# A product-key expert layer on one core: gate tiles stored and read in pieces, read a group ahead, and four early activation tiles kept for the end of the gates

## The chip, the cores and the metric

The kernel runs on one core of a Trainium2 chip. The metric is the device time of one execution in microseconds (us). A core has a matrix engine (PE), a vector engine (DVE), a scalar engine (ACT), a general engine (POOL) and a queue engine (SP) that issues most DMAs. All engines take their instructions in order and wait on semaphores. PE writes to PSUM; everything else here lives in SBUF or, as scratch, in HBM.

## The reference

One decoder layer over 512 tokens of width 1024: a gated token mixer, then an expert network with 16,384 experts, then a last norm. The change touches only the expert network. For each token and each of 8 heads, two small key searches give 16 expert indices and 16 softmax weights.

```python
idx = jnp.take_along_axis(cand_i, pos, axis=-1)
g = jax.nn.softmax(top_s, axis=-1)
u_sel = jnp.take(expert_u, idx, axis=0)
act = jax.nn.gelu(jnp.einsum('thkd,td->thk', u_sel, xc).astype(jnp.float32))
v_sel = jnp.take(expert_v, idx, axis=0)
return jnp.einsum('thk,thkd->td', (g * act).astype(xc.dtype), v_sel)
```

## The kernel before

The first 500 us are the mixer, which the change leaves alone. Of the 512 tokens, 384 (three blocks of 128) go through a dense form of the expert network and 128 through row gathers.

**Dense form.** The experts are cut into 128 tiles of 128. `act_tile(j)` multiplies tile j of `ut` (expert_u transposed, 512 KB) with the normed tokens: 24 matmuls of 384 columns, then a gelu on ACT. `out_tile(j)` takes these activations, multiplies them on DVE with the gates of the tile (`L638`), splits the product into a high and a low part (`w_hi` on ACT, `w_lo` on DVE), loads the expert_v part of `uv` (512 KB) and adds 18 matmuls of 512 columns to the six accumulators that stand in PSUM through all 128 tiles. Every weight passes `weights()`: a load into one of four `raw` buffers, `whi` on ACT (`L74`), `wlo` on DVE or POOL (`L75`), each with three buffers.

**Gates.** The softmax weights are turned into a dense matrix tokens x 16,384 in 48 blocks of 8 tokens: one-hot matrices on DVE (`rows_of`, `L564` and `L566`), 16 matmuls on PE, an eviction on ACT into `stg` (`L585`). After each 4 blocks, 32 tokens, the whole `stg` of 2 MB goes to HBM (`gscr`, `L592`). The second stage reads the gates back by expert tile: `gt` holds all 384 tokens for `JG` = 4 tiles, 768 KB, in runs of 4 x 32 tokens x 4 bytes = 512 bytes (`L634`). Two `gt` buffers stand in turn, and the read stands in the code at the first tile that needs it.

**Tiles ahead of the gates.** `NL` = 74 of the activation tiles (the list `LAG`) don't need the gates and are made earlier, so that PE has work while DVE searches and builds one-hots: `AR` = 20 in the key search, `AD` = 4 after the decode of each of three token blocks, and the other 42 spread over the 48 gate blocks. The first 12 stay in SBUF (`keep`), the other 62 are written to HBM (`ascr`) and read back (`back`, `L661`) `PRE` = 2 tiles ahead into `PRE` + 2 buffers of 192 KB. `wlo` of the first 20 is made on POOL, of the others on DVE.

**Gathers.** For the last 128 tokens, `gathered(i)` reads 128 rows of 8 KB (1 MB) by an indirect DMA of POOL (`L402`), and DVE makes a dot product and a weighted sum. 24 of the 128 steps are spread over the gate blocks, the rest over the second stage.

**Order.** The program is written tile by tile, but a scheduler sets the order on each engine by its own estimates; DMAs of SP go out in that order, one queue, each waiting for its buffer and for the DMA eight places before it, whose semaphore it uses again. The second stage is the loop over j in 0 to 128: `read_back`, `act_tile` where it wasn't made before, `out_tile` of the tile before, and a share of the gathers. At its end `finish` norms the three token blocks.

Of the kernel before, what the change touches and what calls it, by code (L numbers as in the profile page):

```python
# [11 lines left out]
F32 = mybir.dt.float32  # L12
F32R = mybir.dt.float32r
F16 = mybir.dt.float16
BF16 = mybir.dt.bfloat16
I32 = mybir.dt.int32
U32 = mybir.dt.uint32
AF = mybir.ActivationFunctionType
# [3 lines left out]
P = 128  # L22
D = 1024
S = 512
KD = D // P
# [7 lines left out]
NT = ND // P  # L33
EPS = 1e-6
TE = 8
TG = 32
NG = ND // TG
JG = 4
NL = 74
LAG = [j for j in range(P) if j * NL // P != (j - 1) * NL // P]  # L40
JK = 12
GSC = 32768.0
# [3 lines left out]
NS = 2  # L46
AR = 20
AD = 4
UP = 24
PRE = 2  # L50
C_VEC = dict(nm=0, nf=8, ca=16, rw=40, rb=80, brg=90, big=100, lam=110)
NVEC = 120

# [2 lines left out]
def layer(ctx: ExitStack, tc: tile.TileContext, a):  # L56
# [21 lines left out]
    def weights(src, k, eng=None):  # L78
        raw = ring.tile([P, k * P], F32, tag="raw", name="raw", bufs=4)
        SP.dma_start(raw, src)  # L80
        hi, lo = split(raw, [P, k * P], ("whi", "wlo"), ring, 3, eng)
        return hi.rearrange("p (k m) -> p k m", k=k), lo.rearrange("p (k m) -> p k m", k=k)
# [28 lines left out]
    gscr = dram.tile([NG, P, P, TG], F32, name="gscr")  # L111
# [255 lines left out]
    kept = {}  # L367

    def act_tile(j):
        u = weights(a["ut"][j], KD, G if j in LAG[:AR] else V)  # L370
        pa = bank("01", (P, S))
        mm3(pa[:, :ND], u, n2d)
        if j in LAG[:JK]:
            g = gp.tile([P, ND], F32, tag="keep", name="keep", bufs=JK)
        else:
            g = gp.tile([P, ND], F32, tag="gel", name="gel", bufs=3)
        A.activation(g, pa[:, :ND], AF.Gelu_apprx_tanh)
        return g
# [3 lines left out]
    def lag_tiles(n):  # L382
        for _ in range(n):
            j = next(ahead_of_gates, None)
            if j is None:
                return
            kept[j] = act_tile(j)
            if j not in LAG[:JK]:
                SP.dma_start(ascr[j], kept[j])
# [9 lines left out]
    def gathered(i, pin=False):  # L399

        r = gp.tile([P, 2 * D], F32, tag="row", name="row", bufs=4)
        ins = G.indirect_dma_start(  # L402
            out=r, out_offset=None, in_=a["uv"], in_offset=bass.IndirectOffsetOnAxis(ap=uidx[:, i : i + 1], axis=0)
        )
        if pin:
            tc.keep_in_program_order(ins)
        junk = gp.tile([P, D], BF16, tag="junk", name="junk", bufs=1)
        tc.keep_in_program_order(
            V.scalar_tensor_tensor(junk, r[:, :D], 1.0, n2tok, op0=ALU.mult, op1=ALU.mult, accum_out=dots[:, i : i + 1])  # L409
        )  # L410
        A.activation(dots[:, i : i + 1], dots[:, i : i + 1], AF.Gelu_apprx_tanh)
        A.activation(dots[:, i : i + 1], dots[:, i : i + 1], AF.Copy, scale=gk[:, i : i + 1])
        if lastrow:
            gathered_sum()
        lastrow.append((i, r))
# [135 lines left out]
    with tc.tile_pool(name="gates", bufs=1) as rp:  # L551

        ioR = rp.tile([P, P, 2], F16, name="ioR")
        G.iota(ioR, pattern=[[1, P], [0, 2]], base=0, channel_multiplier=0, allow_small_or_imprecise_dtypes=True)
        TP = TE // 2

        def rows_of(t, t0):
            def bc(x):
                return x[:, t0 : t0 + TE].rearrange("p (q t) -> p q t", t=2).unsqueeze(2).to_broadcast([P, TP, P, 2])

            e12 = rp.tile([P, 2, TP, P, 2], F16, tag="e12", name="e12", bufs=2)
            ehl = rp.tile([P, 2, TP, P, 2], F16, tag="ehl", name="ehl", bufs=2)
            for s in range(2):
                V.tensor_tensor(e12[:, s], ioR.unsqueeze(1).to_broadcast([P, TP, P, 2]), bc(iT[t][:, s]), op=ALU.is_equal)  # L564
            for s in range(2):
                V.tensor_mul(ehl[:, s], e12[:, 0], bc(gT[t][:, s]))  # L566
            return e12[:, 1], ehl[:, 0], ehl[:, 1]

        blocks = [(t, t0) for t in range(NT) for t0 in range(0, P, TE)]
        ahead = rows_of(*blocks[0])  # L570
        for n, (t, t0) in enumerate(blocks):
            e2, eh, el = ahead
            if n + 1 < len(blocks):
                ahead = rows_of(*blocks[n + 1])
            c, s0 = divmod(t0, TG)
            if s0 == 0:
                stg = rp.tile([P, P, TG], F32, tag="stg", name="stg", bufs=2)
            for q4 in range(TE // 4):
                pg = bank("4567")
                for i in range(4):  # L580
                    o = pg[:, i * P : (i + 1) * P]
                    ti = 4 * q4 + i
                    T.matmul(o, e2[:, ti // 2, :, ti % 2], eh[:, ti // 2, :, ti % 2], start=True, stop=False)  # L583
                    T.matmul(o, e2[:, ti // 2, :, ti % 2], el[:, ti // 2, :, ti % 2], start=False, stop=True)  # L584
                A.activation(  # L585
                    stg[:, :, s0 + 4 * q4 : s0 + 4 * q4 + 4],
                    pg.rearrange("p (t i) -> p i t", t=4),
                    AF.Copy,
                    scale=1.0 / GSC,
                )  # L590
            if s0 + TE == TG:
                SP.dma_start(gscr[t * (P // TG) + c], stg)  # L592
            left = NL - AR - AD * NT
            lag_tiles((n + 1) * left // len(blocks) - n * left // len(blocks))
            for i in range(n * UP // len(blocks), (n + 1) * UP // len(blocks)):
                gathered(i)


    ep = ctx.enter_context(tc.tile_pool(name="exp", bufs=1))
# [9 lines left out]
                acc[t][k // 4][:, c : c + P], hk[:, t * P : (t + 1) * P], ident, start=False, stop=False, skip_group_check=True  # L609
            )  # L610

    def finish(t, parts):
        sq = ep.tile([P, S], F32, tag="fsq", name="fsq", bufs=2)
        ss = ep.tile([P, 2], F32, tag="fss", name="fss", bufs=2)
        A.activation(sq, parts[0], AF.Square, accum_out=ss[:, 0:1])
        A.activation(sq, parts[1], AF.Square, accum_out=ss[:, 1:2])
        s1 = ep.tile([P, 1], F32, tag="fs1", name="fs1", bufs=2)
        V.tensor_add(s1, ss[:, 0:1], ss[:, 1:2])
        A.activation(s1, s1, AF.Sqrt, bias=epst, scale=1.0 / D)
        V.reciprocal(s1, s1)  # L620
        o = ep.tile([P, D], F32, tag="fo", name="fo", bufs=2)
        for f in range(2):
            fs = slice(f * S, (f + 1) * S)
            V.scalar_tensor_tensor(o[:, fs], parts[f], s1, gfin[:, fs], op0=ALU.mult, op1=ALU.mult)
            SP.dma_start(a["out"][t * P : (t + 1) * P, fs], o[:, fs])

    nout = 0
    gst = {}

    def out_tile(j, g):  # L630
        nonlocal nout
        if j % JG == 0:
            gst["g"] = ep.tile([P, NG, JG, TG], F32, tag="gt", name="gt", bufs=2)
            SP.dma_start(gst["g"], gscr[:, :, j : j + JG, :].rearrange("c p j t -> p c j t"))  # L634
        gt = gst["g"][:, :, j % JG, :]
        v = weights(a["uv"][j * P : (j + 1) * P, D:], KD, V)
        vf = [x.rearrange("p k m -> p (k m)") for x in v]
        V.tensor_mul(g.rearrange("p (c t) -> p c t", t=TG), g.rearrange("p (c t) -> p c t", t=TG), gt)  # L638
        w = split(g, [P, ND], ("w_hi", "w_lo"), ep, 2)
        passes = [(x, y, f) for x, y in ((0, 0), (0, 1), (1, 0)) for f in range(2)]  # L640
        if nout == P - 1:
            passes.sort(key=lambda p: p[2])
        for t in range(NT):
            for x, y, f in passes:
                T.matmul(  # L645
                    acc[t][f],
                    w[x][:, t * P : (t + 1) * P],
                    vf[y][:, f * S : (f + 1) * S],
                    start=nout == 0 and (x, y) == (0, 0),
                    stop=nout == P - 1 and (x, y) == (1, 0),  # L650
                    skip_group_check=True,
                )
        nout += 1
# [8 lines left out]

    work = [lambda i=i: gathered(i) for i in range(UP, HK)]
    work.append(gathered_sum)
    work.append(lambda: finish(3, [yg[:, :S], yg[:, S:]]))
    share = [1.0 if j in LAG else RN for j in range(P)]
    total = sum(share[:-5])
    done = 0
# [2 lines left out]
    for j in range(P + 1):  # L671
        if j < P:
            read_back(j + PRE)
            g = kept[j] if j in LAG else act_tile(j)
            part += share[j]
        if prev is not None:
            out_tile(*prev)
        if 8 <= j < 8 + 2 * KD and j % 2 == 0:
            residual(j // 2 - 4)
        prev = (j, g)  # L680
        while done < min(len(work), math.ceil(part * len(work) / total)):
            work[done]()
            done += 1
    for t in range(NT):
        finish(t, acc[t])


def tiles(w, k, m):
# [46 lines left out]
```

## Time and profile before

| what | value |
|---|---|
| median of 3 runs | 1809.44 us (1804.33 to 1810.34) |
| the profiled execution's own time | 1809.08 us |
| its span, first to last instruction | 1807.4 us |
| PE busy | 1736.7 us (96%) |
| DVE / ACT / POOL busy | 71% / 42% / 18% |
| granted PE clock, mean | 0.984 of 2.4 GHz |
| HBM read / written | 366.93 MB / 41.55 MB |
| reads of `gt` | 32 of 768 KB |
| stores of `stg` | 12 of 2 MB |

The profile is of one execution. Its own time is 1.7 us more than its span, and 0.4 us less than the median. Stretches are named in us from the span's start: the key search and decode run to about 763, the gate blocks to 981, the second stage from there on.

### The profile page before, as it was taken

To read this page: it belongs to the slowest core of one execution; us is meant where nothing else is said; L and a number is where in the kernel's file an instruction comes from. 1 tells how busy PE (TensorE), PEld (TensorE's weight loads), DVE (VectorE), ACT (ScalarE), POOL (GpSimd) and SP (SyncE) were. 2 spreads that over 40 slices of the span, in tenths; PEclk is the share of its full clock that TensorE was granted. 3 is DMA by queue.
4 is the path that set the end of the run, shared out by engine and by line. 5 is a ranking of instruction groups with operands and counts; after the bars stand their busy time and mean duration, and the time that the engine had idled before them with its cause. 6 is when DMAs were issued, how large, how long until landed. Compare 5 with 4: busy or idle time off the path is not lost.

```text
span 1807.4 us, 24072 instructions
## 1 busy us (share of the span) xinstructions
PE 1736.7 (96%) x8861; PEld 1515.1 (84%) x8861; DVE 1286.5 (71%) x2345; ACT 763.8 (42%) x1290; POOL 320.2 (18%) x253
## 2 busy tenths in 40 slices
PE   8999999999989998999999899999899999999998
PEld 6888888888879887999999688788787878888786
DVE  7979442225578668899997777787676866787673
ACT  5774332222343335555554343344343433444353
POOL 0000000000145552023222111122121111122100
PEclk9999999999999998999999999999999999999999
DMA  4323223333433335579999988898898988898872
GB/s 164 114 82 111 96 79 95 107 105 94 134 114 96 103 120 199 171 307 357 376 367 369 347 309 312 297 332 313 283 322 295 323 289 309 310 344 313 308 239 72
DMA packets 147846, 410.06 MB, mean 227 GB/s; under 512 B 11536, under 2 KB 78864, under 8 KB 129680
## 3 DMA queue, kind: packets, MB, share of 16 engines
q1 hardware_dynamic: 129296, 274.30, 45.5%
q0 software_dynamic: 18432, 134.23, 19.2%
q8 instruction: 69, 1.13, 0.2%
q14 instruction: 49, 0.40, 0.1%
HBM read 366.93 MB, written 41.55 MB: 226 GB/s over the span
## 4 chain that ended last, share of the span: by engine, by line
PE 78%; DMA 9%; DVE 8%; issue 2%; ACT 2%; SPq 0%; DVEq 0%; ACTq 0%
PE ps L89 55%; PE acc L645 19%; DMA back<-ascr 5%; DMA gt<-gscr 3%; DVE wlo L75 3%; PE ps L583 1%; PE ps L584 1%; PE ps L517 1%; ACT whi L74 1%; PE ps L236 1%; DVE gel L638 1%; DMA gscr<-stg 1%; ACT w_hi L74 1%; DVE junk L409 1%; DVE nk L141 0%
## 5 line engine op out<-in xcount | busy, mean ns | idle before, releaser
L74 ACT ACTIVATE whi<-raw 128x1024 fp32r<-128x1024 f32 (+1 forms) x364 | 380.6, 1046 | 693.9 <-PE ps L89 479.5
L75 DVE TENSOR_TENSOR wlo<-raw,whi 128x1024 fp32r<-128x1024 f32 (+1 forms) x328 | 393.0, 1201 | 219.1 <-ACT whi L74 218.5
L89 PE MATMUL ps<-q_hi,whi 128*128 128x384 f32 (+1 forms) x1232 | 436.4, 354 | 11.6 <-ACT whi L74 8.9
L89 PE MATMUL ps<-q_hi,wlo 128*128 128x384 f32 (+1 forms) x1232 | 430.0, 349 | 6.1 <-DVE wlo L75 6.1
L89 PE MATMUL ps<-q_lo,whi 128*128 128x384 f32 (+1 forms) x1232 | 429.8, 349 | 0.3 <-DVE q_lo L143 0.3
L402 POOL DMA_INDIRECT row<-uv,uidx x128 | 210.2, 1642 | 766.9 <-DVE yg L396 757.5
L645 PE MATMUL acc<-whi,w_hi 128*128 128x512 f32 x768 | 245.9, 401 | 37.9 <-ACT w_hi L74 37.3
L89 PEld LDWEIGHTS ps<-q_hi,whi 128*128 128x128 f32 x1232 | 234.6, 190 | 24.3 <-ACT whi L74 10.2
L89 PEld LDWEIGHTS ps<-q_hi,wlo 128*128 128x128 f32 x1232 | 234.2, 190 | 17.1 <-DVE wlo L75 8.1
L89 PEld LDWEIGHTS ps<-q_lo,whi 128*128 128x128 f32 x1232 | 234.8, 191 | 11.1 <-DVE q_lo L143 0.7
L645 PE MATMUL acc<-wlo,w_hi 128*128 128x512 f32 x768 | 241.6, 396 | 0.0
L645 PE MATMUL acc<-whi,w_lo 128*128 128x512 f32 x768 | 240.9, 395 | 0.0
L645 PEld LDWEIGHTS acc<-whi,w_hi 128*128 128x128 f32 x768 | 144.9, 192 | 70.8 <-ACT w_hi L74 45.6
L645 PEld LDWEIGHTS acc<-wlo,w_hi 128*128 128x128 f32 x768 | 147.6, 192 | 32.2
L645 PEld LDWEIGHTS acc<-whi,w_lo 128*128 128x128 f32 x768 | 146.5, 191 | 31.5
L89 PE MATMUL ps<-n_hi,whi 128*128 128x512 f32 x432 | 168.4, 390 | 0.0
L89 PE MATMUL ps<-n_hi,wlo 128*128 128x512 f32 x432 | 168.2, 390 | 0.0
L89 PE MATMUL ps<-n_lo,whi 128*128 128x512 f32 x432 | 168.1, 389 | 0.0
L396 DVE SCALAR_TENSOR_TENSOR yg<-row,dots,yg 128x1024 f32<-128x1024 f32 x128 | 163.9, 1280 | 0.0
L409 DVE SCALAR_TENSOR_TENSOR junk<-row,n2tok 128x1024 bf16<-128x1024 f32 x128 | 156.0, 1219 | 0.0
L75 POOL TENSOR_TENSOR wlo<-raw,whi 128x1024 fp32r<-128x1024 f32 x36 | 87.2, 2424 | 349.8 <-ACT whi L74 349.8
L89 PEld LDWEIGHTS ps<-n_hi,wlo 128*128 128x128 f32 x432 | 81.1, 188 | 17.5 <-DVE wlo L75 0.4
(208 smaller groups left out, 1891.7 us busy)
## 6 DMA issues: line engine op xcount, KB each, us to landing
raw<-ut SPq DMA_DIRECT2D x128, 512.0 KB
raw<-uv SPq DMA_DIRECT2D x128, 512.0 KB
raw<-w_in SPq DMA_DIRECT2D x60, 512.0 KB
gscr<-stg SPq DMA_DIRECT2D x12, 2048.0 KB
gt<-gscr SPq DMA_DIRECT2D x32, 768.0 KB
ascr<-gel SPq DMA_DIRECT2D x62, 192.0 KB
back<-ascr SPq DMA_DIRECT2D x62, 192.0 KB
raw<-w_q SPq DMA_DIRECT2D x16, 512.0 KB
```

The costliest lines, as they stand in the source:

```text
L74: A.activation(hi, raw, AF.Copy)
L75: (lo_eng or V).tensor_sub(lo, raw, hi.bitcast(F32))
L89: T.matmul(ps, w[x][:, i, :], r[y][i], start=first and n == 0, stop=last and n == 3 * k - 1)
L236: T.matmul(pg, x[:, s * P : (s + 1) * P], y, start=n == 0, stop=n == 2)
L396: V.scalar_tensor_tensor(yg, r[:, D:], dots[:, i : i + 1], yg, op0=ALU.mult, op1=ALU.add)
L402: ins = G.indirect_dma_start(out=r, out_offset=None, in_=a["uv"], in_offset=bass.IndirectOffsetOnAxis(ap=uidx[:, i : i + 1], axis=0))
L409: V.scalar_tensor_tensor(junk, r[:, :D], 1.0, n2tok, op0=ALU.mult, op1=ALU.mult, accum_out=dots[:, i : i + 1])
L517: T.matmul(psc[:, s * P : (s + 1) * P], qs[s][:, t * P : (t + 1) * P], keys[:, 2 * hd + s, :], start=True, stop=True)
L583: T.matmul(o, e2[:, ti // 2, :, ti % 2], eh[:, ti // 2, :, ti % 2], start=True, stop=False)
L584: T.matmul(o, e2[:, ti // 2, :, ti % 2], el[:, ti // 2, :, ti % 2], start=False, stop=True)
L638: V.tensor_mul(g.rearrange("p (c t) -> p c t", t=TG), g.rearrange("p (c t) -> p c t", t=TG), gt)
L645: T.matmul(acc[t][f], w[x][:, t * P : (t + 1) * P], vf[y][:, f * S : (f + 1) * S], start=nout == 0 and (x, y) == (0, 0), stop=nout == P - ...
```

## The change

Seven edits. `JG` goes from 4 to 8: `gt` holds 8 tiles, 12 KB per partition and buffer, in runs of 1,024 bytes. Each read of it is cut into six pieces of 2 x 32 tokens, 256 KB each; they stand in the code one group ahead of the use, at the tiles 1 to 6 of the group before (`read_gates`). The store of `stg` is cut into four pieces of 512 KB, at most two issued at a gate block. `NL` goes from 74 to 76, and `AT` = 4 of these tiles are taken out of the gate blocks, which now have 40, and stand behind the last store. `PRE` goes from 2 to 3, with 5 `back` buffers. `wlo` of the four tiles after the first decode is made on POOL instead of DVE. `finish` squares into its own output buffer and keeps the three outputs in one `gt` buffer.

```diff
-JG = 4
-NL = 74
+JG = 8
+NL = 76
+AT = 4
-PRE = 2
+PRE = 3
...
-        u = weights(a["ut"][j], KD, G if j in LAG[:AR] else V)
+        u = weights(a["ut"][j], KD, G if j in LAG[:AR + AD] else V)
...
             if s0 + TE == TG:
-                SP.dma_start(gscr[t * (P // TG) + c], stg)
-            left = NL - AR - AD * NT
+                stores += [
+                    lambda i=i, c=t * (P // TG) + c, stg=stg: SP.dma_start(gscr[c, :, i : i + P // 4, :], stg[:, i : i + P // 4, :])
+                    for i in range(0, P, P // 4)
+                ]
+            for _ in range(2):
+                if stores:
+                    stores.pop(0)()
+            left = NL - AR - AD * NT - AT
             lag_tiles((n + 1) * left // len(blocks) - n * left // len(blocks))
             for i in range(n * UP // len(blocks), (n + 1) * UP // len(blocks)):
                 gathered(i)
+        while stores:
+            stores.pop(0)()
+        lag_tiles(AT)
...
+    def read_gates(n, c0, c1):
+
+        if n * JG >= P:
+            return
+        if c0 == 0:
+            gst[n] = ep.tile([P, NG, JG, TG], F32, tag="gt", name="gt", bufs=2)
+        SP.dma_start(gst[n][:, c0:c1], gscr[c0:c1, :, n * JG : (n + 1) * JG, :].rearrange("c p j t -> p c j t"))
+
     def out_tile(j, g):
         nonlocal nout
-        if j % JG == 0:
-            gst["g"] = ep.tile([P, NG, JG, TG], F32, tag="gt", name="gt", bufs=2)
-            SP.dma_start(gst["g"], gscr[:, :, j : j + JG, :].rearrange("c p j t -> p c j t"))
-        gt = gst["g"][:, :, j % JG, :]
+        k = j % JG
+        if j == 0:
+            for c in range(0, NG, 2):
+                read_gates(0, c, c + 2)
+        if 1 <= k <= NG // 2:
+            read_gates(j // JG + 1, 2 * k - 2, 2 * k)
+        gt = gst[j // JG][:, :, k, :]
...
+    fo = ep.tile([P, NG, JG, TG], F32, tag="gt", name="fo", bufs=2).rearrange("p c j t -> p (c j t)")
     for t in range(NT):
-        finish(t, acc[t])
+        o = fo[:, t * D : (t + 1) * D]
+        finish(t, acc[t], o, o)
```

Where it moves instructions is shown at two places. The first is the end of the gates. On ACT, before, the last two evictions into `stg` are followed by three gelus (`gel<-ps`, one for each activation tile), and then by the first `w_hi`, which needs the gates.

```order
L585 ACTIVATE stg_9040<-ps_9222 128x128x4
L585 ACTIVATE stg_9040<-ps_9232 128x128x4
L74 ACTIVATE whi_9376<-raw_9374 128x1024
L377 ACTIVATE gel_9274<-ps_9249 128x384
L74 ACTIVATE whi_9412<-raw_9410 128x1024
L377 ACTIVATE gel_9334<-ps_9309 128x384
L74 ACTIVATE whi_9445<-raw_9443 128x1024
L377 ACTIVATE gel_9441<-ps_9416 128x384
L74 ACTIVATE w_hi_9345<-keep_3983 128x384
L74 ACTIVATE w_hi_9381<-gel_9334 128x384
```

On ACT, now, from just behind the last eviction; the first `w_hi` is the next row, and the gelu of a sixth tile stands three rows further.

```order
L75 ACTIVATE whi_9322<-raw_9320 128x1024
L378 ACTIVATE gel_9240<-ps_9215 128x384
L75 ACTIVATE whi_9356<-raw_9354 128x1024
L378 ACTIVATE gel_9283<-ps_9258 128x384
L412 ACTIVATE dots_3822<-dots_3822 128x1
L413 ACTIVATE dots_3822<-dots_3822,gk_3821 128x1
L75 ACTIVATE whi_9409<-raw_9407 128x1024
L378 ACTIVATE gel_9317<-ps_9292 128x384
L75 ACTIVATE whi_9449<-raw_9447 128x1024
L378 ACTIVATE gel_9351<-ps_9326 128x384
L75 ACTIVATE whi_9487<-raw_9485 128x1024
L378 ACTIVATE gel_9385<-ps_9360 128x384
```

PE has, behind its last gate matmul, three activation tiles before and six now. On SP, before, at the same place: the last store of 2 MB, then `gfin` (a constant of 512 KB that needs the space of the gate buffers), then two reads of `gt`.

```order
L80 DMA raw_9479<-uv 128x1024
L592 DMA gscr_78<-stg_9040 128x4096
L389 DMA ascr_79<-gel_9274 128x384
L80 DMA raw_9515<-ut 128x1024
L601 DMA gfin_9288<-nfin 128x1024
L634 DMA gt_9336<-gscr_78 128x12x128
L634 DMA gt_9548<-gscr_78 128x12x128
```

On SP, now: the last store in four pieces with a spill of the first of the six tiles between them, then `gfin`, then the six pieces of the first `gt`.

```order
L595 DMA gscr_78<-stg_9003 128x1024 x2
L390 DMA ascr_79<-gel_9240 128x384
L595 DMA gscr_78<-stg_9003 128x1024 x2
L390 DMA ascr_79<-gel_9283 128x384
L81 DMA raw_9485<-uv 128x1024
L612 DMA gfin_9392<-nfin 128x1024
L645 DMA gt_9440<-gscr_78 128x2x256
L390 DMA ascr_79<-gel_9317 128x384
L645 DMA gt_9440<-gscr_78 128x2x256 x4
L390 DMA ascr_79<-gel_9351 128x384
L645 DMA gt_9440<-gscr_78 128x2x256
```

The last store and the first read keep their order; what moved is the number of activation tiles beside them.

The second place is a change of group in the second stage, on SP. Before, the read of `gt_12812` stands four weight loads ahead of `raw_12814`, the `uv` part of the first tile that uses it (the last row).

```order
L634 DMA gt_12812<-gscr_78 128x12x128
L661 DMA back_12739<-ascr_79 128x384
L80 DMA raw_12703<-uv 128x1024
L661 DMA back_12777<-ascr_79 128x384
L80 DMA raw_12741<-uv 128x1024
L80 DMA raw_12779<-ut 128x1024
L80 DMA raw_12814<-uv 128x1024
```

Now, the pieces of `gt_12348` (the group of the tiles 64 to 71); the `uv` part of tile 64 is the load that follows the last row shown.

```order
L645 DMA gt_12348<-gscr_78 128x2x256 x5
L81 DMA raw_12452<-uv 128x1024
L681 DMA back_12488<-ascr_79 128x384
L645 DMA gt_12348<-gscr_78 128x2x256
L81 DMA raw_12491<-uv 128x1024
L81 DMA raw_12527<-ut 128x1024
L681 DMA back_12597<-ascr_79 128x384
L81 DMA raw_12561<-uv 128x1024
L681 DMA back_12665<-ascr_79 128x384
L81 DMA raw_12600<-uv 128x1024
L81 DMA raw_12636<-uv 128x1024
L81 DMA raw_12667<-ut 128x1024
```

The read moved from 2 to 5 weight loads ahead of the first user, over the groups behind the first two, to 8 to 10 for its first piece and 7 to 9 for its last. `back`, but for the first few, moved from 5 to 7 loads ahead of its tile's `uv` part to 7 to 10.

## Rows read from the trace of the kernel before

**Rows 1.** The page: busy time of PE, and its granted clock in 40 slices

```profile
PE 1736.7 (96%) x8861; PEld 1515.1 (84%) x8861; DVE 1286.5 (71%) x2345; ACT 763.8 (42%) x1290; POOL 320.2 (18%) x253
...
PEclk9999999999999998999999999999999999999999
```

**Rows 2.** Who waited for whom, 1005 to 1800: us in total, times, longest

```profile
DVE back L638 <- DMA back<-ascr: 42.3, 13, 5.9
...
PE acc L645 <- ACT w_hi L74: 37.3, 13, 8.2
DVE back L638 <- DMA gt<-gscr: 37.1, 17, 5.3
...
DVE keep L638 <- DMA gt<-gscr: 7.9, 3, 4.8
...
DVE back L638 <- DMA raw<-uv: 4.1, 1, 4.1
```

**Rows 3.** The same view for the SP queue's own waits

```profile
SPq L661 <- DVE w_lo L75: 88.6, 32, 5.2
```

**Rows 4.** The chain that ended last, in order of time: start, us, what

```profile
802.28 4.22 PE ps L89 x24
807.44 4.22 PE ps L89 x24
...
976.03 4.06 PE ps L89 x23
982.83 13.18 DMA gscr<-stg
996.54 2.20 DMA gt<-gscr
1005.67 18.43 PE acc L645 x72
...
1084.42 4.16 PE ps L89 x24
1088.58 8.17 PE acc L645 x36
...
1288.33 11.41 DMA back<-ascr
1302.61 6.20 PE acc L645 x18
...
1786.15 8.87 PE acc L645 x39
```

**Rows 5.** Busy us (instructions) of each engine by stretch, granted clock, DMA share, GB/s

```profile
1005.67:1795.02 789.35, 759.68 (x3586) 659.35 (x3587) 578.13 (x745) 315.15 (x569) 145.38 (x100) 0.98 0.85 298
...
1600.00:1700.00 100.00, 99.36 (x475) 86.23 (x474) 78.35 (x101) 42.44 (x78) 23.33 (x15) 1.00 0.94 327
1700.00:1795.00 95.00, 90.81 (x425) 78.39 (x424) 56.74 (x73) 37.95 (x61) 4.30 (x3) 0.98 0.53 180
```

**Rows 6.** Groups of PE by line and form, 1006 to 1795: the residual's matmuls

```profile
L608 PE MATMUL acc<-ident,hk 128*128 128x128 f32 x48 | 6.6, 274 | 0.0
```

**Rows 7.** A stretch of the gate blocks, columns as in rows 5

```profile
860.00:880.00 20.00, 20.00 (x159) 19.52 (x158) 19.95 (x28) 10.22 (x21) 2.29 (x2) 1.00 1.02 408
```

**Rows 8.** Waits from 690 to 765, columns as in rows 2

```profile
PE ps L89 <- DVE wlo L75: 4.7, 2, 3.5
```

**Rows 9.** Groups by line: `wlo` on POOL (whole span) and on DVE (765 to 982)

```profile
L75 POOL TENSOR_TENSOR wlo<-raw,whi 128x1024 fp32r<-128x1024 f32 x36 | 87.2, 2424 | 349.8 <-ACT whi L74 349.8
...
L75 DVE TENSOR_TENSOR wlo<-raw,whi 128x1024 fp32r<-128x1024 f32 x42 | 51.3, 1221 | 4.5 <-ACT whi L74 4.2
```

**Rows 10.** The page's DMA part: all packets, then SP's queue and the gathers' queue

```profile
DMA packets 147846, 410.06 MB, mean 227 GB/s; under 512 B 11536, under 2 KB 78864, under 8 KB 129680
...
q1 hardware_dynamic: 129296, 274.30, 45.5%
q0 software_dynamic: 18432, 134.23, 19.2%
```

More of the change, by code (lines that the diff above doesn't have):

```diff
@@ L570, in layer @@
         ahead = rows_of(*blocks[0])
+        stores = []
         for n, (t, t0) in enumerate(blocks):
@@ L610, in residual, with finish @@
             )
[L612 to L617, printed above, removed]
+    def finish(t, parts, o, junk):
+        ss = ep.tile([P, 2], F32, tag="fss", name="fss", bufs=3)
+        for f in range(2):
+            A.activation(junk[:, f * S : (f + 1) * S], parts[f], AF.Square, accum_out=ss[:, f : f + 1])
+        s1 = ep.tile([P, 1], F32, tag="fs1", name="fs1", bufs=3)
         V.tensor_add(s1, ss[:, 0:1], ss[:, 1:2])
@@ L620, in finish @@
         V.reciprocal(s1, s1)
-        o = ep.tile([P, D], F32, tag="fo", name="fo", bufs=2)
         for f in range(2):
@@ L664, in layer @@
     work.append(gathered_sum)
-    work.append(lambda: finish(3, [yg[:, :S], yg[:, S:]]))
+    work.append(lambda: finish(3, [yg[:, :S], yg[:, S:]], yg, gp.tile([P, D], BF16, tag="junk", name="junk", bufs=1)))
     share = [1.0 if j in LAG else RN for j in range(P)]
```

## The prediction

> **What bounds the kernel now.** I read the page first: PE is busy for 96% of the span and the granted clock is near full in nearly all of it [rows 1]. So the question is where the other 4% lies. The busy time by stretch puts 789.35 - 759.68 = 29.7 us of PE's idle time into the second stage, from its first accumulating matmul (1005.67) to its last (1795.02) [rows 5]. The waits name what ends it: PE waits for `w_hi` 13 times, 37.3 us in all, the longest 8.2 us [rows 2]. `w_hi` needs the product with the gates, and DVE waits there for the reads of `back` (42.3 us) and of `gt` (37.1 and 7.9 us) [rows 2]; not all of that reaches PE. SP in turn waits 88.6 us for `w_lo` before it may issue a `back`: the read goes out when one of four buffers comes free, too late [rows 3].
>
> The chain in order of time shows both places. At the end of the gates: PE's last tile to 980.1, the 2 MB store from 982.83 for 13.18 us, the `gt` read from 996.54, and PE again at 1005.67 [rows 4]. In the second stage: a `back` of 11.41 us at 1288.33, and PE at 1302.61 [rows 4]. The reader should also see the price behind a stall: 18 matmuls took 6.20 us there, while 36 take 8.17 us undisturbed (4.09 for 18) [rows 4]. PE runs slow for a while after it has stood still.
>
> **How much there is to win.** A tile of activations takes 4.16 us, a tile of outputs 8.17 / 2 = 4.085 us [rows 4], the residual 6.6 us in all [rows 6]. The second stage has 52 and 128 of them: 216.3 + 522.9 + 6.6 = 745.8 us. It takes 789.35: 43.5 us too much. The waits explain 37.3 - 8.2 = 29.1 us; the remaining 14.4 us is slow running behind the twelve waits, 1.2 us each.
>
> **The change, part by part.**
>
> *Gate blocks.* A block with a tile takes 5.16 us (802.28 to 807.44), of which the tile is 4.22 [rows 4], so 0.94 is the block's own. Now the last block ends at 980.1 + 0.9 = 981.0. The blocks lose two tiles: PE saves 8.4 us. DVE is as full as PE (19.95 of 20 us) [rows 7]; it saves 2 x 1.22 us for their `wlo`, and four `wlo` more, 4.9 us, go to POOL [rows 9], where they cost 9.7 us of an engine that is free there (2.29 of 20 us) [rows 7]. That is 7.3 us of DVE against 8.4 us of PE. Bounds: 2.4 us earlier, if the relief before the blocks doesn't carry over; 8.4 + 4.7 = 13.1 us, if PE's waits for `wlo` in the decode go too [rows 8] and DVE keeps up. I take 8.4, since PE is what the blocks wait for today: they end at 972.6.
>
> *Behind the gates.* PE now has six tiles there, 25.0 us, to 997.6. Beside them run the store and the read. The first pieces go out 1.8 us after the blocks' end, as now (982.83 - 981.0): 974.4. The last two stand behind the spill of the first of the six tiles, so some 5 us later. With the 13.18 us of today's 2 MB [rows 4] the data has landed between 987.6 and 992.7. From the read's issue to the first product's use it was 1005.67 - 996.54 = 9.1 us [rows 4], with 2 MB in front (two `gt` of 768 KB and the 512 KB of `gfin`); the same 2 MB (six pieces and `gfin`) stand there now. So the gates are ready between 996.7 and 1001.8, and PE between 0 and 4.2 us late. I take 1.5 us: the first accumulating matmul at 999.1, with 51 activation tiles left instead of 52. The gain there is 6.6 + 4.2 = 10.8 us.
>
> *Second stage.* `gt` is read 7 to 10 weight loads ahead instead of 2 to 5, `back` 7 to 10 instead of 5 to 7. A load is used every 789 / 180 = 4.4 us, so `gt` goes out some 20 us earlier and `back` some 9 us earlier. The longest waits on them were 5.3 and 5.9 us [rows 2]. Both lists of waits should go. What stays I take from the stretch 1600 to 1700, where PE had 0.64 us idle in 100 [rows 5]: 4.8 us over 750, and 1.2 us of slow running: 6 us. Bounds: 0, and today's 43.5. The two more spills and reads (192 KB each) lie beside other work.
>
> *End.* From PE's last matmul to the end: 1807.4 - 1795.0 = 12.4 us. `finish` has the same instructions on the same engines; only buffers change. I take it as unchanged, between 1 us less and 1 us more.
>
> *Sum.* 999.1 + 51 x 4.16 (212.2) + 522.9 + 6.6 + 6 + 12.4 = 1759.2 us of span. The profiled execution took 1.7 us more than its span, and the median is 0.4 us above it: **1761 us**, against 1809.4.
>
> **DMA, the resource that could deny it.** In the second stage the DMA engines are busy for 0.85 of 789 us = 671 us. The last 95 us have 0.53, 50 us; the first 694 us have 621 us, 0.895 [rows 5]. With PE unhindered those 694 us shrink to about 656, and the same transfers need a share of 0.95. The 512-byte runs become 1,024-byte runs, so 32 x 768 KB / 512 = 49,152 packets become half as many. What a packet costs beyond its bytes is bounded by the two queues: SP's takes 0.455 x 1807.4 x 16 / 274.3 = 48.0 us of one engine for a MB, the gathers' with 8 KB packets 41.4 [rows 10]. The difference, over all of SP's 129,296 packets, is 14 ns each; 24,576 fewer save at most 21.5 us of all sixteen, at least nothing. I take half, 11 us: a share of 0.93. The stretch 1600 to 1700 ran at 0.94 with PE busy for 99.4%, and 860 to 880 above that with PE full [rows 5, 7]. So I expect it to hold.
>
> **Rivals.**
>
> *A. DMA stays at today's share.* If 0.895 is what this mix of reads can have, the first 694 us need (621 - 11) / 0.895 = 682 us, and only 12 us are won there instead of 38 or more: 1809.4 - 10.8 - 12 = 1787 us; 1799 without the packets' relief, 1775 with all of it. The waits would then stand on weight loads and on POOL's rows. For it: the mean share is already high, and some waits may stem from that. Against it: the two stretches above. The case that pieces still arrive late, since SP is one queue in order, ends in the same range (nothing won in the stage is 1799).
>
> *B. Six pieces at once push the weight loads back.* At 14 changes of group SP issues up to 1.5 MB in a row, ahead of loads that are needed next. At 327 GB/s [rows 5] that is 4.8 us, twice today's 2.4 us for 768 KB. If each burst stood fully on the path, with 1.2 us of slow running behind it, it would cost 14 x 6.0 = 84 us: 1845 us, slower. The point from which it decides is 48 / 14 = 3.5 us a burst. Against it: today's 32 bursts of half the size led to a single wait that names a weight load, 4.1 us [rows 2], and `whi` has three more buffers between load and PE.
>
> The Trainium skill speaks against pieces too: DMA: Bandwidth & Descriptors, Bandwidth, asks for DMAs of at least 1 MiB, and by the fit that its section Anatomy of one DMA gives for POOL's queue, 2.0 us plus bytes / 436 GB/s, six pieces of 256 KB would take 15.6 us against 7.6 for two reads of 768 KB, 8.0 us more at each of 14 changes if they ran one after another, an estimate of 1761 + 112 = 1873 us. With that rule, which is the far end of B and has 0.02 of its chance, the trace does not agree: the 1600 to 1700 stretch moved 327 GB/s with no SP transfer above 768 KB [rows 5].
>
> *C. The gate blocks are bound by DVE alone.* Then they end 2.4 us earlier instead of 8.4, the rest as in the sum: 1767 us. This lies in the forecast's own range.
>
> **How the numbers follow.** Chances: the forecast, with C and with a left-over of 0 to 16 us, 0.60 (1747 to 1771); better still, with PE's whole gain in the decode, 0.06; A 0.22 (1771 to 1799); B 0.12 (above 1799). The range 1746 to 1792 holds the forecast's 0.60 and its better edge, and most of A, together about 0.8. Within 0.3%, 5.4 us of 1809.4, is what a measurement of this kernel can't tell from no change: 1804 to 1815. B spreads around that: 0.02 faster, 0.05 same, 0.05 slower. Faster: 0.60 + 0.06 + 0.22 + 0.02 = 0.90.
>
> **What would show it.** Right: no wait of PE above 2 us behind the gates; the waits of DVE for `gt` and `back` nearly gone; SP's wait for `w_lo` before `back` shorter, or without effect; PE at 99% in the second stage with a DMA share of 0.92 to 0.94; the first accumulating matmul near 999. Wrong: new waits of ACT (`whi`) for `raw` behind each group's pieces would be B; a DMA share of 0.90 with waits spread over loads and rows would be A; gaps of PE inside the gate blocks, with DVE full, would be C.

## The result and the profile after

| kernel | median, us | runs | ratio to before, 95% interval |
|---|---|---|---|
| before | 1807.04 | 4 (1804.33 to 1810.34) | |
| changed | 1855.63 | 4 (1847.03 to 1865.76) | 1.027 [1.0213, 1.0327] |

The change makes the kernel 2.7% slower; the forecast was 1761 us, 2.7% faster. The profiled execution took 1853.93 us. Its page, against [rows 1, 10]: PE is busy for 9 us more in all and the same number of instructions, and the packets of SP's queue have fallen by 17,792: the gates' reads have 24,576 fewer, as the prediction counted, and the store in pieces (6,144 packets of 4 KB in place of 1,536 of 16 KB) with some smaller transfers gives 6,784 back.

```profile
PE 1746.0 (94%) x8861; PEld 1519.5 (82%) x8861; DVE 1287.3 (70%) x2341; ACT 766.5 (41%) x1290; POOL 417.0 (23%) x257
...
PEclk9999999999999998999999999999999999999999
...
DMA packets 130055, 410.86 MB, mean 222 GB/s; under 512 B 13200, under 2 KB 56464, under 8 KB 113424
...
q1 hardware_dynamic: 111504, 275.09, 44.5%
```

The waits of the second stage, 1000 to 1845 (us in total, times, longest), answer to [rows 2]:

```profile
ACT w_hi L75 <- DVE gel L658: 165.1, 52, 9.4
...
DVE back L658 <- DMA back<-ascr: 89.8, 31, 5.0
...
PE acc L665 <- ACT w_hi L75: 72.8, 26, 7.2
...
DVE back L658 <- DMA raw<-uv: 31.4, 6, 9.2
DVE keep L658 <- DMA gt<-gscr: 18.5, 2, 9.5
DVE back L658 <- DMA gt<-gscr: 17.3, 3, 8.3
DVE back L658 <- DMA raw<-ut: 8.5, 1, 8.5
...
ACT whi L75 <- DMA raw<-uv: 4.1, 2, 2.4
```

Neither of DVE's two lists has gone. It stands 89.8 us for `back`, against 42.3, and by the names in this view 35.8 us for `gt` (17.3 and 18.5), against 45.0; the landing times below put more of it on `gt`. PE stands 72.8 us for `w_hi`, against 37.3. The weight loads are not what is late: `whi` waits for `raw` 4.1 us in all.

Busy time by stretch, columns as in [rows 5, 7]:

```profile
1005.32:1840.00 834.68, 765.59 (x3563) 660.06 (x3564) 578.85 (x746) 315.89 (x570) 145.58 (x100) 0.97 0.80 283
...
1500.00:1600.00 100.00, 87.03 (x406) 74.55 (x405) 68.43 (x88) 36.91 (x68) 18.19 (x13) 0.97 0.83 296
...
860.00:880.00 20.00, 19.70 (x167) 18.94 (x166) 20.00 (x29) 11.37 (x22) 16.28 (x3) 1.00 0.91 334
```

The second stage took 834.7 us, against 789.35: the 45 us that the span grew by are all there. DMA's share fell to 0.80. A queue of transfers that was too full would show the opposite.

One stall at close range. The timeline of the changed kernel, 1373.2 to 1389.3 (start, duration, engine, what, and in brackets the idle time before it and what ended it):

```profile
1373.61 0.35 SPq L681 DMA_DIRECT2D back<-ascr  x1
1374.02 0.42 SPq L645 DMA_DIRECT2D gt<-gscr  x1
...
1375.84 1.22 DVE L76 TENSOR_TENSOR wlo<-raw,whi 128x1024 fp32r<-128x1024 f32 x1
...
1378.46 0.47 ACT L378 ACTIVATE gel<-ps 128x384 f32<-128x384 f32 x1
...
1381.11 0.61 PE L665 MATMUL acc<-whi,w_lo 128*128 128x512 f32 x2
1386.16 0.56 DVE L658 TENSOR_TENSOR back<-back,gt 128x384 f32<-128x384 f32 x1 [9.10 <-DMA raw<-uv]
1386.64 1.22 DVE L76 TENSOR_TENSOR wlo<-raw,whi 128x1024 fp32r<-128x1024 f32 x1
1387.77 0.55 DVE L658 TENSOR_TENSOR gel<-gel,gt 128x384 f32<-128x384 f32 x1
1387.88 0.33 SPq L81 DMA_DIRECT2D raw<-ut  x1
1388.36 0.52 ACT L75 ACTIVATE w_hi<-gel 128x384 fp32r<-128x384 f32 x1 [9.42 <-DVE gel L658]
...
1388.93 0.79 PE L665 MATMUL acc<-whi,w_hi 128*128 128x512 f32 x1 [7.21 <-ACT w_hi L75]
```

DVE has nothing to do for 9.10 us but to wait in front of a product of a `back`, which nobody needs yet. Behind it in its queue stands the product of `gel`, whose input ACT made at 1378.46; ACT's `w_hi` waits 9.42 us for it and PE 7.21 us. The name in the bracket, `raw<-uv`, is not what was waited for. The landing of the two reads at the top of the fence, `back` at 1373.61 and the piece of `gt` at 1374.02 (each of one transfer, us from its issue):

```profile
DMA to landing us min/median/max: 10.4/10.4/10.4
...
DMA to landing us min/median/max: 12.0/12.0/12.0
```

So `back` was there at 1384.0 and the last piece of the next group's gates at 1386.0, and the product began at 1386.16. Comparing each late product in this way with the landing of its two inputs gives 93.0 us (28 times) to the product's own `back`, and 56.5 us (12 times, up to 9.2) to the last piece of `gt`: 149.5 us in all, where the four rows of `back L658` above sum to 147.0.

### The profile page after: what moved, and what is told of

It reads as the page before. It is cut to its first block, busy times and chain, and to the rows that moved or that the text cites. A ratio compares the mean times of both kernels' runs of the same rounds, so it can differ in the third digit from the quotient of the medians.

```text
span 1852.2 us, 24212 instructions
## 1 busy us (share of the span) xinstructions
PE 1746.0 (94%) x8861; PEld 1519.5 (82%) x8861; DVE 1287.3 (70%) x2341; ACT 766.5 (41%) x1290; POOL 417.0 (23%) x257
## 3 DMA queue, kind: packets, MB, share of 16 engines
q0 software_dynamic: 18432, 134.23, 18.8%
## 5 line engine op out<-in xcount | busy, mean ns | idle before, releaser
L76 DVE TENSOR_TENSOR wlo<-raw,whi 128x1024 fp32r<-128x1024 f32 (+1 forms) x324 | 387.2, 1199 | 187.8 <-ACT whi L75 187.7
L403 POOL DMA_INDIRECT row<-uv,uidx x128 | 292.9, 2289 | 723.8 <-DVE yg L397 719.1
L665 PE MATMUL acc<-whi,w_hi 128*128 128x512 f32 x768 | 249.4, 406 | 72.8 <-ACT w_hi L75 72.8
L665 PEld LDWEIGHTS acc<-whi,w_hi 128*128 128x128 f32 x768 | 146.1, 195 | 109.1 <-ACT w_hi L75 83.7
L76 POOL TENSOR_TENSOR wlo<-raw,whi 128x1024 fp32r<-128x1024 f32 x40 | 98.5, 2467 | 357.4 <-ACT whi L75 357.4
L658 DVE TENSOR_TENSOR back<-back,gt 128x384 f32<-128x384 f32 x64 | 35.1, 555 | 150.2 <-DMA back<-ascr 89.8
```

The source lines that it names most:

```text
L76: (lo_eng or V).tensor_sub(lo, raw, hi.bitcast(F32))
L403: ins = G.indirect_dma_start(out=r, out_offset=None, in_=a["uv"], in_offset=bass.IndirectOffsetOnAxis(ap=uidx[:, i : i + 1], axis=0))
L665: T.matmul(acc[t][f], w[x][:, t * P : (t + 1) * P], vf[y][:, f * S : (f + 1) * S], start=nout == 0 and (x, y) == (0, 0), stop=nout == P - ...
```

## The experiments

**What the order says.** In the stall above nothing passed the product in 9.10 us: DVE took its instructions in the order in which the scheduler put them. The Trainium skill (PSUM — Partial Sum Buffer, Engine vs sequencer instructions) calls the vector queue a strict FIFO, and the trace agrees with it. Counted in the built order, the product of a `back` stood 24.8 DVE instructions ahead of the `w_lo` split of the same tile before (16 to 33), and stands 38.4 ahead of it now (28 to 68). In the traces the time from the product's end to its `w_hi` grew from 27.2 to 44.8 us, and that from the issue of the read to the product's start shrank from 12.6 to 7.5 us (means without the first five, which are read far ahead). A `back` takes 6.6 us to land, in the median, and up to 12.3.

**Theory 1**: the scheduler puts the product as early as its own estimate lets the inputs be there, and DVE then stands in front of it. Before, the product had to come behind a `gt` that was read late, and that gave `back` time to land; with the gates read a group ahead this brake is gone. The trace of the kernel before agrees in part. By the ends of the packets (512 bytes for `gt`, 1,536 for `back`) 17 of its late products, 40.8 us, waited for `gt`, with their `back` there for 8 us or more; 12, 42.0 us, waited for `back` even then. **Theory 2**: the pieces, issued in bursts, make transfers late. **Theory 3**: the reads are not early enough. Ten kernels bear on them.

**a_pin**: the changed kernel with the product kept in the order of the program, beside its use ("the pin").

```diff
-        V.tensor_mul(g.rearrange("p (c t) -> p c t", t=TG), g.rearrange("p (c t) -> p c t", t=TG), gt)
+        tc.keep_in_program_order(
+            V.tensor_mul(g.rearrange("p (c t) -> p c t", t=TG), g.rearrange("p (c t) -> p c t", t=TG), gt)
+        )
```

> The changed kernel with one thing more: the product of a tile with its gates (L658 on DVE) keeps its place in the program instead of the scheduler's, some 2 DVE instructions ahead of the split that uses it instead of some 38. All reads and their sizes stay. Theory 1 (DVE, in order, stands at products that were placed right behind their reads, long before PE needs them): the waits of DVE for back and gt fall from 89.8 and 35.8 us to under 15 us each, and the time to 1755 to 1785 us. Theory 2 (the pieces and bursts make every transfer land too late): the waits only move to the place of use, and the time stays within 15 us of the changed kernel's 1855.

1756.42 us, ratio 0.9694 [0.9671, 0.9717]. The waits, 1000 to 1745 (the last row is the SP queue's own), and three stretches:

```profile
DVE keep L659 <- DMA gt<-gscr: 8.6, 1, 8.6
...
PE acc L667 <- ACT w_hi L75: 3.6, 1, 3.6
...
SPq L683 <- DVE w_lo L76: 88.2, 52, 4.1
```

```profile
1002.66:1658.00 655.34, 655.34 (x3158) 574.64 (x3159) 528.59 (x678) 284.69 (x512) 154.24 (x98) 1.00 0.92 337
1002.66:1742.00 739.34, 739.34 (x3561) 648.08 (x3562) 581.35 (x747) 321.15 (x569) 157.60 (x100) 1.00 0.87 320
...
1500.00:1600.00 100.00, 100.00 (x482) 87.76 (x481) 81.64 (x105) 43.57 (x79) 23.76 (x15) 1.00 0.92 338
```

The 3.6 us are PE's wait before its first accumulating matmul, called the entry from here on; in the 739 us behind it PE has no gap at all. The same pieces, in the same sizes, are read at a higher rate, 338 GB/s, and a `back` lands as late as it did (6.3 us in the median, up to 12.7). So neither the pieces nor DMA's rate cost the 100 us: the place of the products on DVE did. The pin also moves some reads on SP by a few rows, since the scheduler works out all queues together; the landing times show that they didn't get faster by it. SP still waits 88.2 us for `w_lo` before it may issue a `back`, as long as the 88.6 us of [rows 3], and it costs nothing.

**b_pin**: the kernel before with the same three lines, nothing else of the change.

> The kernel before with the same one edit: products in the program's order (some 2 DVE instructions ahead of the split instead of some 25). Theory 1: the wait for back (42.3 us) goes, as the product now stands some 25 us later; the reads of gt stay late (45 us of DVE's waiting), since they go out only 2 to 5 loads ahead, so the time falls by 10 to 30 us, to 1777 to 1797. Theory 2 says nothing of the kernel before, and expects no more than 5 us.

1761.74 us, ratio 0.9722 [0.9699, 0.9745]. It gained more than the 10 to 30 us that I had expected: not only the waits for `back` went, but those for `gt` too, since with the product beside its use `gt` is read early enough as it is. What is left to PE, 1000 to 1745, is the entry alone:

```profile
DVE keep L639 <- DMA gt<-gscr: 5.5, 1, 5.5
...
PE acc L647 <- ACT w_hi L74: 8.9, 1, 8.9
```

**a_pre2** is the changed kernel with `PRE` = 2, **b_pre3** the kernel before with `PRE` = 3.

```diff
-PRE = 3
+PRE = 2
...
-PRE = 2
+PRE = 3
```

> The changed kernel with PRE = 2 and four back buffers, as before; all else as changed. The products stand some 30 DVE instructions ahead of their use instead of 38 (25 in the kernel before). Theory 1: with products less early, the wait for back lies between 42 and 90 us, and the time between 1790 and 1840 us. Theory 2: the pieces are unchanged, so the time stays at 1840 to 1870.

> The kernel before with PRE = 3 and five back buffers alone. The products stand where they stood (25 DVE instructions ahead), and the read goes out a tile earlier. Theory 1: the wait for back falls from 42.3 us to under 20 us, and the time by 5 to 20 us. Theory 2: no more than 5 us either way, since no piece is changed.

a_pre2: 1839.67 us, ratio 1.0157 [1.0132, 1.0182]; b_pre3: 1769.81, ratio 0.9765 [0.9737, 0.9792]. The waits of a_pre2, and then of b_pre3:

```profile
DVE back L658 <- DMA back<-ascr: 124.0, 39, 8.6
...
PE acc L665 <- ACT w_hi L75: 61.5, 25, 6.5
```

```profile
DVE back L638 <- DMA gt<-gscr: 45.7, 18, 5.5
PE acc L645 <- ACT w_hi L74: 12.8, 4, 8.3
...
DVE back L638 <- DMA back<-ascr: 2.4, 1, 2.4
```

Both missed what I had expected. a_pre2 waits 124.0 us for `back`, where I had at most 90, and its time lies at the end of one theory's range and 0.3 us from the other's, so it doesn't tell them apart. b_pre3 fell by 40 us against its own before (1810.26), where I had 5 to 20. The earlier `back` helps where the late `gt` holds the products (25.0 rows ahead of the split, issue to product 22.0 us), and makes things no better where nothing holds them (30.3 rows with `PRE` = 2, 38.4 with 3; 7.0 and 7.5 us). b_pre3 also shows which wait was dear before: DVE still stands 45.7 us for `gt`, and PE, but for the entry's 8.3 us, lost only 4.5.

**b_gates** is the kernel before with the gates read a group ahead alone (`JG` = 8, `read_gates`, `finish` as in the change); **b_tail** is the kernel before with the other part alone (`NL` = 76, `AT` = 4, the store in pieces).

```diff
-JG = 4
+JG = 8
...
+        if 1 <= k <= NG // 2:
+            read_gates(j // JG + 1, 2 * k - 2, 2 * k)
```

```diff
-NL = 74
+NL = 76
+AT = 4
...
-                SP.dma_start(gscr[t * (P // TG) + c], stg)
+                stores += [
...
+        lag_tiles(AT)
```

> The kernel before with one part of the change alone: JG = 8 and the gates read a group ahead in six pieces (with finish keeping its outputs in a gt buffer, for space); back still two tiles ahead, NL = 74, the store uncut. Theory 1 (the late read of gt held the products back; without it the scheduler places each product close behind its read of back, and in-order DVE stands there): this part alone makes the kernel slow. The products stand about 31 rows ahead of their split on DVE, against 24.8 before: 1825 to 1850 us, DVE waiting for back 80 us or more, for gt under 25, PE waiting for w_hi 50 us or more. Theory 2 (a third buffer ahead for back, with five buffers instead of four, or the kept tiles, do it): 1765 to 1800, since gt no longer waits and nothing else changed.

> The kernel before with the other part alone: NL = 76, four tiles kept for the end of the gates, the store in four pieces; the gates read late and whole, back two tiles ahead. Theory 1: the second stage stays as before (products about 25 rows ahead of their split, waits of DVE for gt and back some 35 to 45 us each, of PE for w_hi behind the entry 25 to 35), and only the entry gains: 1798 to 1808. Theory 2 (kept tiles and store pieces are what costs): 1815 or more, with the first accumulating matmul at 1006 or later.

b_gates: 1848.94 us, ratio 1.0211 [1.0155, 1.0268]; b_tail: 1806.51, ratio 0.9976 [0.9952, 1.0001]. The waits of b_gates, and then of b_tail:

```profile
DVE back L647 <- DMA back<-ascr: 129.2, 34, 9.2
PE acc L654 <- ACT w_hi L74: 70.2, 25, 8.8
```

```profile
DVE back L649 <- DMA back<-ascr: 54.6, 18, 6.7
DVE back L649 <- DMA gt<-gscr: 44.6, 16, 6.6
...
PE acc L656 <- ACT w_hi L75: 38.9, 14, 6.7
```

Reading the gates early, alone, makes nearly all of the loss; the kept tiles and the cut store are worth 0.2%, with an interval that reaches to no change at all. Products stand 31.7 and 24.9 rows ahead of their split in the two. The waits of b_tail for `back` (54.6 us, expected 35 to 45) and of PE (38.9, expected 25 to 35) are longer than I had written; they are of its profiled execution, the longest of ten, 1812.92 us.

**a_pre5** is the changed kernel with `PRE` = 5, and so seven `back` buffers.

```diff
-PRE = 3
+PRE = 5
```

> The changed kernel with back read five tiles ahead into seven buffers. Theory 1 (the product follows its read, wherever the read stands, since the scheduler places it by its own estimate of when the data lands): the products move ahead with the reads (49 rows ahead of their split instead of 38), DVE stands as often: 1835 to 1865, DVE waiting for back 70 us or more. Theory 3 (the reads are simply not early enough, and two tiles more would cover the 6.6 us that they take to land): 1755 to 1780, waits for back under 15 us.

1855.12 us, ratio 1.0241 [1.0183, 1.0299], the time that Theory 1 had, and Theory 3 falls. The split among the waits, 1000 to 1845, is not as I had written:

```profile
DVE back L658 <- DMA raw<-uv: 41.2, 6, 9.4
DVE back L658 <- DMA back<-ascr: 33.9, 12, 4.5
DVE back L658 <- DMA gt<-gscr: 30.4, 5, 9.2
...
DVE back L658 <- issue: 12.1, 2, 9.5
```

Together 117.6 us, but `back` is less than a third of it. The packets in the trace (1,024 bytes for `gt`, 1,536 for `back`) tell what the others waited for. Before 13 of the late products, 83.7 us of waiting, the last packet of the tile's `gt` ended 0.5 to 1.0 us before the product began, and the last of its `back` 16 us or more before it. Before the other 12, 33.9 us, it was the product's own `back`, 0.4 to 0.7 us before. So the products did move ahead (49.6 rows), but not as far as their reads: 18.8 us lie between issue and product, against 7.5. What most of them then stand at is the last `gt` piece of the next group, as in the stall shown above. Theory 3 is right in that a `back` read earlier is waited for less; it gains nothing, since DVE stands at the other input instead.

**What the rest is worth once the products stand right.** b_tail_pin is b_tail with the three lines of the pin; a_pin_at5 is a_pin with `NL` = 77 and `AT` = 5; a_pin_dve is a_pin with `wlo` of the four tiles back on DVE (of the last two the diffs):

```diff
-NL = 76
+NL = 77
-AT = 4
+AT = 5
...
-        u = weights(a["ut"][j], KD, G if j in LAG[:AR + AD] else V)
+        u = weights(a["ut"][j], KD, G if j in LAG[:AR] else V)
```

> The kernel before with the four kept tiles, NL = 76, the store in four pieces, and the product kept in the order of the program; gates read late, whole, four tiles at a time, and back two tiles ahead. It differs from the pinned changed kernel (1756.4) by what reads the gates and back earlier, and by wlo of four tiles on POOL. Theory 1 (once the products stand beside their use, how early gt and back are read no longer matters): 1752 to 1758, PE's waits in the second stage behind the entry under 3 us. Theory 3 (reading the gates and back earlier is worth something by itself): 1762 or more, with waits of DVE for gt or back of 10 us or more.

> The changed kernel with the product kept in the order of the program, and a fifth tile kept for the end of the gates (NL = 77, AT = 5). If PE's 3.6 us at the entry is the store and the read of gt being longer than the tiles beside them: that wait goes, and 1751 to 1755. If the entry waits for something else that moves with the tiles: as without the fifth tile, 1756 or more.

> The pinned changed kernel (1756.4) with wlo of the four tiles behind the first decode back on DVE. If that part of the change is what my sum took it for (it frees DVE by 1.22 us each, and PE's waits for wlo in the decode go): 1758 to 1763, with PE waiting 4.4 us for a wlo near 711. If it moves PE's decode waits only from wlo to other instructions (after it: 2.5, 3.6 and 1.5 us for gelu and selection instead): 1754 to 1758, the end of the gate blocks within 2 us.

| kernel | median, us | ratio, 95% interval |
|---|---|---|
| b_tail_pin | 1754.37 | 0.9698 [0.9679, 0.9717] |
| a_pin_at5 | 1754.85 | 0.969 [0.9638, 0.9743] |
| a_pin_dve | 1756.07 | 0.971 [0.9693, 0.9727] |

The four kernels with the pin and kept tiles lie within 2.1 us, and each is faster than both kernels of this study. b_tail_pin reads `back` two tiles ahead and the gates late and whole, and PE waits only at the entry, in all (1000 to 1745):

```profile
PE acc L658 <- ACT w_hi L75: 3.1, 2, 1.9
```

So reading earlier is worth nothing here once DVE no longer stands, and pinned products with kept tiles are the version to keep, if by little: b_pin, without kept tiles, has 0.9722, and its interval overlaps theirs. The fifth tile took no more than 1.6 us: PE's one wait of 3.6 us became two of 3.9 us together, so its time fell within what I expected of the wait's going, but the wait stayed. `wlo` on POOL instead of DVE is worth nothing that can be measured; the decode's 4.4 us wait for `wlo`, which a_pin_dve was to bring back if POOL had removed it, came back as 4.8 us in all (2 times, up to 3.5), and the time didn't change.

## Why the prediction was wrong, step by step

**The step that failed** is "Both lists of waits should go." It counted how far ahead of its own tile's weight load a read goes out, and took the product to stand at its tile. It doesn't: on DVE it stands where the scheduler puts it, and the same edit that moved the reads moved the products further. The read of a `back` went out 12.5 us earlier against its use (52.9 us from its issue to the tile's `w_hi`, against 40.4), more than the 9 us I had worked out, but the product 17.6 us earlier (44.8 - 27.2), so 5.1 us of slack were lost (12.6 - 7.5). That the scheduler's estimate puts landings too early is inferred from the orders; its numbers are in no view. The row that could have told me stood in [rows 2]: DVE waited up to 5.9 us for a `back` that goes out 5 to 7 loads, 22 us or more, ahead of its tile's use. A read that late in landing would be strange; a consumer that early is the simpler reading. I also took SP's 88.6 us of waiting before a `back` [rows 3] for the reason that `back` is late; a_pin has 88.2 us of it and no late `back`.

**Second stage.** I had 6 us left over; the stage lost 94.9 us against a_pin (834.6 - 739.7, to the start of `finish`). 68.8 us are PE's 25 waits behind 1010, and 765.6 - 739.3 = 26.3 us is the slow running behind them, 1.05 us each where I had 1.2; the mean granted clock of the stage is 0.97 against 1.00. The chain shows the price again, 18 matmuls in 6.80 us behind an 11.66 us read:

```profile
1747.94 11.66 DMA back<-ascr
...
1762.46 6.80 PE acc L665 x18
```

**Gate blocks.** The last evictions begin at 976.57, before 981.44: 4.9 us earlier where I took 8.4, inside my bounds of 2.4 and 13.1. DVE is full and PE not (20.00 and 19.70 of 20 us), the sign that I wrote down for rival C, but the gain lies between C's 2.4 us and the sum's 8.4. The size is within what the end moves by between kernels whose code differs only behind it: 974.26 in a_pin, and 975.47 in b_tail_pin against 971.97 in b_tail.

**Behind the gates.** First accumulating matmul at 1005.32, not 999.1; PE stood 4.00 us, not 1.5, inside my bounds of 0 and 4.2. Of the 6.2 us by which it came later, 2.5 are this wait and 3.5 the gate blocks. The wait term was mis-sized: from the first piece's issue to the first use it took 1005.32 - 992.01 = 13.3 us, where I had carried over 9.1 from the read in one. The pieces stand in one queue with spills, and the sixth went out 6.6 us after the first (998.57). In b_gates, where the six go out within 2.5 us, it took 10.1 us.

**DMA.** The share fell, since DVE's stall also keeps loads waiting for buffers (SP issues nothing between 1377.1 and 1387.9 in the stall above). That the chip can carry the reads at PE's full speed held: a_pin has a share of 0.92 over the 655 us from its first accumulating matmul, where I had 0.93 over about 656. **End.** 1852.2 - 1839.9 = 12.3 us, as forecast.

**The sum itself** was about right for a kernel whose products stand at their tiles: 1759.2 us of span forecast, 1754.6 in a_pin. It has one error of reading. 1795.02 is where the chain leaves PE, not PE's last matmul; in the kernel before, 15 matmuls, 3.38 us, still run behind it, beside `finish`:

```profile
1795.02:1799.00 3.98, 3.38 (x15) 2.45 (x14) 0.40 (x3) 3.88 (x9) 0.00 (x0) 1.00 0.00 0
```

The sum counts them twice, in the 128 tiles and in the 12.4 us of the end. Without that it gives 1755.8 us.

**Rivals.** A (DMA's share) and B (bursts) are refuted by a_pin, which has the same transfers. B's number, 1845, lay near the result for another reason. The wait of 4.1 us that names a weight load in [rows 2], which I held against B, stands in front of a product of a `back`, which takes no weights; in the stall above the same name was wrong. The rule of at least 1 MiB (the Trainium skill, DMA: Bandwidth & Descriptors, Bandwidth), from which the prediction had its estimate of 1873, is not what bound here: a_pin moved 338 GB/s with transfers of at most 512 KB on SP's queue beside the gathers' 1 MB. No rival of mine had DVE's in-order queue as its mechanism. C moved the result by at most the 3.5 us that the gate blocks gained less.

## What to carry to other kernels

On an engine that takes its work in order, an instruction that waits for a DMA and is placed long before its result is needed holds up everything behind it; so look not at how early a read goes out, but at what stands behind its first consumer on that engine. When a late input is made early, ask what it was holding back, and where a scheduler will now put the consumer. A name that ends a wait is to be checked against landing times when it makes no sense as an input of the waiting instruction.

## What the runs showed of the hardware

POOL's issue of a gather grew. Groups of POOL from 765 to 982, the kernel before and then the changed one (busy, mean ns of one | idle before):

```profile
L402 POOL DMA_INDIRECT row<-uv,uidx x24 | 59.9, 2494 | 167.6 <-DVE yg L396 167.6
```

```profile
L403 POOL DMA_INDIRECT row<-uv,uidx x23 | 142.4, 6193 | 76.4 <-DVE yg L397 76.4
```

The mean is 2.49 us in the four kernels that store `stg` whole, and 5.3 to 6.2 us in the eight that store it in pieces (and keep four or five tiles). It mixes a few fixed lengths, two of them in the changed kernel and one in the kernel before:

```profile
792.42 8.77 POOL L403 DMA_INDIRECT row<-uv,uidx  x1 [7.15 <-DVE yg L397]
804.26 6.36 POOL L403 DMA_INDIRECT row<-uv,uidx  x1 [3.07 <-DVE yg L397]
```

```profile
819.47 1.15 POOL L402 DMA_INDIRECT row<-uv,uidx  x1 [0.66 <-DVE yg L396]
```

The length goes with what DVE does as the issue begins, in all twelve kernels. Beside a `wlo` followed by another `wlo` it is 8.8 us (7 times in each of the eight), beside a `wlo` followed by a one-hot `e` 6.4 us (8 times in the eight, 6 in the four). Beside two `e` it is 1.1 to 1.2 us, but 5.2 us for 3 to 5 issues in five of the eight. So the order on DVE has changed, and most of the growth goes with it rather than with the pieces or the tiles as such; why an issue lasts as long is not shown, nor why some of 5.2 us stand beside `e`. POOL had room for it.
